# Where three groups of low parts are formed: a pointwise weight of the convolution layer behind its sixth chunk, and four splits at the end of attention on GpSimd instead of VectorE

## The chip, the cores and the metric

The kernel runs on one core of a Trainium2 chip. The time is the device time of one execution in microseconds; runs are compared by their medians. The five engines named below are TensorE (PE, with its weight loads as PEld), VectorE (DVE), ScalarE (ACT), GpSimd (POOL) and SyncE (SP, which here only issues transfers).

## The reference

A trunk of two layers works on 512 tokens of width 1024, all in float32. Layer 0 mixes tokens with a Conformer convolution, layer 1 with differential attention of 8 heads. After each mixer stand a SwiGLU FFN and a gated per-layer input `p` of width 256.

```python
def conformer_conv(x, ...):
    a = x @ w_pw1 + b_pw1
    u = a[..., :D] * sigmoid(a[..., D:])
    u = conv_general_dilated(u, dw_w, causal, width 31) + dw_b
    u = silu(layer_norm(u, ln_g, ln_b))
    return u @ w_pw2 + b_pw2

def diff_attention(x, ...):
    q, k, v = split(x @ w_qkv, 3)
    q = rms_norm(q, q_g) * HEAD_DIM ** -0.5;  k = rms_norm(k, k_g)
    # per block of 128 queries, per head
    probs = softmax(q @ k.T + bias, causal)          # two maps per head
    w = probs[:, :, 0] - lam * probs[:, :, 1]
    o = rms_norm(w @ v, sub_g) * (1 - lambda_init)
    return o @ w_o
```

The projection of `p` (`p @ ple_w_proj`, 256 to 1024) doesn't depend on the mixer, so the kernel can do it anywhere in a layer.

## The kernel before

The stream is kept transposed as 8 chunks of 128 features by 512 tokens. Each float32 product is made of three TensorE products: a factor is split into a high part (a rounded copy) and a low part (the value minus the high part), and `mm3` (L160 to L166) adds low by high, high by low and high by high. A weight of 128 by 1024 therefore takes three steps (`weight`, L146): a transfer into one of two `wraw` buffers, ACT's copy `whi` (L157), and a subtraction that gives `wlo` (L159), on DVE unless `eng` says otherwise. The same is done to activations: `z` in the convolution layer (L571 on ACT, L575 on DVE), the attention outputs `A` (L178, L179), and the two halves of `p` (`pfeatures`, L278 and L279).

Each engine works through its own instructions in a fixed order. A planner sets that order when the program is built; in the loop over `z` the order of DVE and ACT is that of the code, and `issue_after` puts an instruction behind another one. An instruction whose operands aren't ready holds up everything behind it on its engine.

Two places matter here.

**The start of the second pointwise product (`w_pw2`, about 150 to 182 us).** For each of 8 chunks DVE shifts (L550, or POOL at L560 for chunks 3 to 7) and multiplies (L568), ACT does silu (L569) and the high part (L571), DVE the low part (L575). `linear` starts three output blocks together, so that each chunk of `z` feeds three weights; the fourth weight follows alone. The planner had put the fourth weight's split among the first chunks.

**The end of attention (about 755 to 805 us).** Work is cut into stages. A unit multiplies tokens by a slab of the q and k weights, scales the result on POOL by the root found there (`r`, L229; `big<-big,r`, L925), and `unit_end` transposes it on PE (L931) and writes the six `C` tiles on ACT, DVE and POOL (L939 to L949). `stage_s` makes the scores (PE L976, L977), which DVE reads from one of two `sc` buffers (L979), ACT exponentiates (L983) and DVE combines (L986 to L988). `stage_t` transposes them (PE L996) and splits them (ACT L998, DVE L999). `stage_a` multiplies by the values (PE L1012, L1013), `stage_o` transposes the outputs (PE L1041). When the last slab is done, the loop over `pp` fills in the projection of `p`: `project` multiplies two weights (`w = weight()`, each used for four output blocks) by the two halves of `p`, with a stage between the pieces.

For a narrow block of queries both maps share one `sc` buffer, so that the second map's matmuls wait until DVE has read the first.

Of the kernel before, what the change touches and what calls it, by code (L numbers as in the profile page):

```python
# [15 lines left out]
ALU = mybir.AluOpType  # L16
# [4 lines left out]
P = 128  # L21
S = 512
D = 1024
NC = D // P
# [68 lines left out]
def trunk(ctx, tc, xT, pT, wts, diag, dww, vec, rel, onehot, lamv, out):  # L93
    nc = tc.nc
    V, A, G, T = nc.vector, nc.scalar, nc.gpsimd, nc.tensor
# [20 lines left out]
    f = lambda ap: ap.bitcast(F32)  # L116
# [6 lines left out]
    def col(name, i=0):  # L123
        a, _ = VEC[name]
        return vt[:, a + i : a + i + 1]
# [17 lines left out]
    wnext = [0]  # L143
    loaded = [None]

    def weight(n=1024, pieces=1, between=(), eng=V, after=None):  # L146
        i = wnext[0]
        wnext[0] += 1
        raw = sb([P, 1024], "wraw", 2)
        hi = sb([P, 1024], "whi", 4, F32R)  # L150
        lo = sb([P, 1024], "wlo", 4, F32R)
        for k in range(pieces):
            cut = slice(k * n // pieces, (k + 1) * n // pieces)
            loaded[0] = nc.sync.dma_start(raw[:, cut], wts[i, :, cut])
            if k < len(between):
                between[k]()
            A.copy(hi[:, cut], raw[:, cut])  # L157
            with tc.issue_after(after.ins) if after else nullcontext():
                eng.tensor_tensor(lo[:, cut], raw[:, cut], f(hi[:, cut]), ALU.subtract)  # L159
        return hi, lo  # L160
# [7 lines left out]
    def wpart(w, k):  # L168
        return tuple(t[:, k * P : (k + 1) * P] for t in w)
# [98 lines left out]
    def pfeatures(layer, parts):  # L268
        for k, (hi, lo) in enumerate(parts):
            if layer == 0:  # L270
                if k == 0:
                    two = sb([P, 2, S], "B7", 1)
                    nc.sync.dma_start(two.rearrange("p a s -> p (a s)"), pT[layer])
                raw = two[:, k]
            else:
                raw = sb([P, 1024], "wraw", 2)[:, :S]
                nc.sync.dma_start(raw, pT[layer, :, k * S : (k + 1) * S])
            A.copy(hi, raw)  # L278
            (G if layer == 0 else V).tensor_tensor(lo, raw, f(hi), ALU.subtract)  # L279
        return parts  # L280


# [11 lines left out]
    y = []  # L294
# [141 lines left out]
    last_add = [None]  # L436
# [77 lines left out]
    def factor(after):  # L514
        m = len(pp)
        if m < 6:
            o = sb([P, S], f"D{m}", 1)
        elif m == 6:
            pw.append(sb([P, 2, S], "C4", 2))
            o = pw[2][:, 0]  # L520
        else:
            o = pw[2][:, 1]
        with tc.issue_after(after[0].ins):
            pp.append(project(ph, m, pw[m // 4], o))
# [34 lines left out]
        for c in range(3, NC):  # L559
            G.tensor_tensor(y[c], y[c], drow, ALU.add)  # L560

    z = []
    with tc.manual_schedule(engines={V.engine, A.engine}):
        for c in range(NC + 1):
            if c < NC:
                if c in (1, 2):
                    shift(c)
                V.tensor_tensor(y[c], y[c], lrow, ALU.mult)  # L568
                A.activation(y[c], y[c], AF.Silu, scale=col("ln_g", c), bias=col("ln_b", c))  # L569
                z.append((sb([P, S], f"A{2 * c}", 1, F32R), sb([P, S], f"A{2 * c + 1}", 1, F32R)))  # L570
                A.copy(z[c][0], y[c])  # L571
                if c < 2:
                    factor(last_product)
            if c >= 1:
                V.tensor_tensor(z[c - 1][1], y[c - 1], f(z[c - 1][0]), ALU.subtract)  # L575

    def linear(n_in, src, consume, group0=1, before=None, after=None, first=(None,) * 3):


        m = 0  # L580
        while m < NC:
            g = group0 if m == 0 else 1
            ws = [weight(n_in * P, after=first[i] if m == 0 else None) for i in range(g)]
            accs = [mm() for _ in range(g)]
            for k in range(n_in):
                if before:
                    before(k)
                for w_, a_ in zip(ws, accs):
                    mm3(a_, wpart(w_, k), src[k], k == 0, k == n_in - 1)
                    if after:  # L590
                        after()
            for i in range(g):
                consume(m + i, accs[i])
            m += g
# [3 lines left out]
    def add_conv(m, acc):  # L598
        V.scalar_tensor_tensor(h[m], acc, col("b_pw2", m), h[m], ALU.add, ALU.add)
        norm.chunk(m)  # L600

    linear(NC, z, add_conv, 3, first=(None, last_add[0], None))


    def ffn(norm, after, space):
# [449 lines left out]
    def take(n):  # L1055
        got, stages[:n] = [s for _, s in stages[:n]], []
        return got

    waiting = None
    for what, at, pace in QKV:  # L1060
        ws = slab(GLO if what == "q" and at > 0 else 0, P * at[1] if what == "v" else S)
        for tb in range(4):
            if (what, at, tb) == ("v", (6, 2), 0):
                ph = pfeatures(1, [both(sb([P, 2, S], t, 1, F32R)) for t in ("B0", "B1")])
            between = take(3 * pace[tb])
# [22 lines left out]
    pp = []  # L1088
    for m in range(NC):
        if m % 4 == 0:  # L1090
            w = weight()
        step()
        if m % 2 == 0:
            o2 = sb([P, 2, S], f"B{m // 2 + 2}", 1) if m < 4 else sb([P, 2, S], f"C{m // 2 + 1}", 2)
        pp.append(project(ph, m, w, o2[:, m % 2], step))
# [155 lines left out]
```

## Time and profile before

| | |
|---|---|
| runs, us | 1257.83, 1261.02, 1260.38 (median 1260.38) |
| profiled execution, us | 1259.05, of which the span 1257.3 |
| busy, share of span | PE 99%, PEld 86%, DVE 72%, ACT 49%, POOL 21% |
| 150 to 182 us: busy of 32.0 | PE 29.95, DVE 19.57, ACT 19.91, POOL 10.47 |
| 754 to 771 us: busy of 17.0 | PE 16.74, DVE 16.75, ACT 14.25, POOL 9.78 |
| 771 to 804 us: busy of 33.0 | PE 28.54, DVE 31.00, ACT 26.81, POOL 4.51 |
| granted TensorE clock | 1.00 in these stretches, 0.95 as the mean of 771 to 804 |

The time of an execution is its span and 1.75 us around it. In the timelines a row has the start, the duration, the engine, the line, the operation with output and inputs, and in brackets how long the engine had stood idle and what ended that. The same form can be longer in one place than in another (a subtraction of 128x1024 on DVE: 1.22 to 2.64 us). Matmuls overlap: three of 128 by 512 in a row start some 0.23 us apart though each lasts 0.40.

### The profile page before, as it was taken

Reading aid. Unit: us, or ns where it says so; the run is one execution under the profiler, and the core shown is the slowest. Engines: PE = TensorE matmul, PEld = TensorE weight load, DVE = VectorE, ACT = ScalarE, POOL = GpSimd, SP = SyncE. Lnnn points to the kernel's source line nnn. Section 1 sums busy time; section 2 is a strip of 40 time slices with the busy share of each in tenths; the row PEclk is TensorE's granted clock in tenths of the full one; section 3 lists DMA queues with packets and bytes.
Section 4 is the critical chain, followed back from the end, with each engine's and each line's share of the span. In section 5 each row is a group of like instructions: output and inputs, shape, how many; then the busy total and the mean of one; then the engine's idle time right before and its main releaser. Section 6 shows DMA issues by size and latency. Waiting matters only on the chain.

```text
span 1257.3 us, 18628 instructions
## 1 busy us (share of the span) xinstructions
PE 1239.1 (99%) x7152; PEld 1086.2 (86%) x7152; DVE 904.6 (72%) x1482; ACT 615.5 (49%) x1023; POOL 264.1 (21%) x231
## 2 busy tenths in 40 slices
PE   9999999999999999999999998999999999999998
PEld 7888778898999899988888987878898999899887
DVE  6998755965588558667678889746965598468665
ACT  6743454543355235446566768634542355235441
POOL 2853522000001000042616633122000000000030
PEclk9999999999999999999999999999999999999999
DMA  8666223464466444243322214223554467444241
GB/s 298 199 194 179 74 76 109 131 164 129 122 176 181 137 110 122 67 147 96 90 92 76 76 48 129 85 67 101 151 156 145 103 182 184 137 109 117 77 134 67
DMA packets 60597, 158.39 MB, mean 126 GB/s; under 512 B 6451, under 2 KB 11059, under 8 KB 60508
## 3 DMA queue, kind: packets, MB, share of 16 engines
q1 hardware_dynamic: 53776, 136.99, 34.3%
q0 software_dynamic: 4608, 16.78, 8.2%
q10 hardware_dynamic: 2124, 3.43, 0.9%
q8 instruction: 56, 0.92, 0.3%
q14 instruction: 33, 0.27, 0.1%
HBM read 151.91 MB, written 4.21 MB: 124 GB/s over the span
## 4 chain that ended last, share of the span: by engine, by line
PE 96%; DVE 2%; ACT 1%; DMA 0%; issue 0%; SPq 0%; ACTq 0%
PE mm L164 26%; PE mm L165 25%; PE mm L166 25%; PE tp L166 2%; PE tp L165 2%; PE tp L164 2%; PE sc L370 2%; PE sc L165 1%; PE sc L166 1%; PE sc L164 1%; PE mm L1012 1%; PE sc L976 1%; PE sc L977 1%; PE tp L996 1%; PE mm L370 1%; PE mm L326 1%
## 5 line engine op out<-in xcount | busy, mean ns | idle before, releaser
L165 PE MATMUL mm<-A,whi 128*128 128x512 f32 (+1 forms) x904 | 311.6, 346 | 0.3 <-DVE A L575 0.3
L164 PE MATMUL mm<-A,wlo 128*128 128x512 f32 (+1 forms) x904 | 307.2, 345 | 4.7 <-DVE wlo L159 3.0
L166 PE MATMUL mm<-A,whi 128*128 128x512 f32 (+1 forms) x904 | 310.0, 343 | 0.0
L157 ACT CAST whi<-wraw 128x1024 fp32r<-128x1024 f32 (+2 forms) x150 | 151.3, 1015 | 225.4 <-PE mm L166 103.8
L159 DVE TENSOR_TENSOR wlo<-wraw,whi 128x1024 fp32r<-128x1024 f32 (+2 forms) x147 | 186.3, 1270 | 61.0 <-ACT whi L157 60.3
L164 PEld LDWEIGHTS mm<-A,wlo 128*128 128x128 f32 x904 | 171.4, 190 | 26.3 <-ACT A L178 2.5
L165 PEld LDWEIGHTS mm<-A,whi 128*128 128x128 f32 x904 | 171.5, 190 | 21.8 <-issue 1.2
L166 PEld LDWEIGHTS mm<-A,whi 128*128 128x128 f32 x904 | 171.6, 190 | 20.8 <-issue 1.4
L165 PE MATMUL mm<-B,whi 128*128 128x512 f32 x368 | 143.3, 390 | 0.0
L166 PE MATMUL mm<-B,whi 128*128 128x512 f32 x368 | 143.3, 390 | 0.0
L164 PE MATMUL mm<-B,wlo 128*128 128x512 f32 x368 | 141.1, 391 | 0.0
L681 POOL DMA_DIRECT2D C<-in_wts x32 | 28.1, 878 | 512.1 <-DVE h L792 178.2
L204 POOL TENSOR_TENSOR acc<-acc,wk 128x512 f32<-128x512 f32 x35 | 56.6, 1617 | 218.3 <-ACT wk L203 110.9
L166 PEld LDWEIGHTS mm<-B,whi 128*128 128x128 f32 x368 | 69.1, 188 | 15.0
L165 PEld LDWEIGHTS mm<-B,whi 128*128 128x128 f32 x368 | 69.1, 188 | 14.3
L164 PEld LDWEIGHTS mm<-B,wlo 128*128 128x128 f32 x368 | 69.1, 188 | 14.2
L166 PE MATMUL mm<-whi,A 128*128 128x512 f32 (+1 forms) x224 | 81.1, 363 | 0.0
L164 PE MATMUL mm<-whi,A 128*128 128x512 f32 (+1 forms) x224 | 80.9, 366 | 0.0
L165 PE MATMUL mm<-wlo,A 128*128 128x512 f32 (+1 forms) x224 | 80.8, 364 | 0.0
L792 DVE TENSOR_TENSOR h<-mm,h 128x512 f32<-128x512 f32 x48 | 33.0, 688 | 64.5 <-PE mm L166 64.5
L229 POOL TENSOR_TENSOR r<-v,mhalf 128x8 f32<-128x8 f32 (+1 forms) x31 | 46.2, 1490 | 120.9 <-DVE v L227 99.9
L674 DVE TENSOR_TENSOR wlo<-wraw,whi 128x1024 fp32r<-128x1024 f32 x32 | 39.2, 1225 | 33.5 <-ACT whi L673 33.4
(271 smaller groups left out, 2674.4 us busy)
## 6 DMA issues: line engine op xcount, KB each, us to landing
wraw<-in_wts SPq DMA_DIRECT2D x162, 512.0 KB, 3.6
C<-in_wts SPq DMA_DIRECT2D x32, 512.0 KB, 4.8
C<-in_wts POOLq DMA_DIRECT2D x32, 512.0 KB, 5.8
bias<-in_wts SPq DMA_DIRECT2D x32, 256.0 KB, 3.2
wraw<-in_wts SPq DMA_DIRECT2D x16, 384.0 KB, 3.1
D<-in_diag SPq DMA_DIRECT2D x22, 256.0 KB, 4.6
C<-in_diag SPq DMA_DIRECT2D x16, 256.0 KB, 4.7
h<-in_xT SPq DMA_DIRECT2D x8, 256.0 KB, 5.4
```

Source lines behind the costliest of these rows:

```text
L157: A.copy(hi[:, cut], raw[:, cut])
L159: eng.tensor_tensor(lo[:, cut], raw[:, cut], f(hi[:, cut]), ALU.subtract)
L164: T.matmul(acc, al, bh, start=first, stop=False)
L165: T.matmul(acc, ah, bl, start=False, stop=False)
L166: return T.matmul(acc, ah, bh, start=False, stop=last)
L204: self.last = self.eng.tensor_tensor(self.acc, self.acc, sq, ALU.add)
L229: last_pow[0] = G.tensor_tensor(r[:, :n], v[:, :n], mhalf[:, :n], ALU.pow)
L326: last_tap[0] = T.matmul(acc, dg[:, j % 4], ups[c][:, j : j + S], start=(j == 0), stop=(j == PE_TAPS[c] - 1))
L370: last_tap[0] = T.matmul(acc[:, g * P : (g + 1) * P], w, ups[c][:, g, LEAD - m : LEAD - m + P], start=(m == 0), stop=(m == LAGS - 1),)
L674: V.tensor_tensor(lo, raw, f(hi), ALU.subtract)
L681: nc.gpsimd.dma_start(q, wts[i + 2].rearrange("p (a s) -> p a s", a=2), accum_op=ALU.add)
L792: V.tensor_tensor(h[m], acc, h[m], ALU.add)
```

## The change

Three edits. (1) `weight()` gets `behind`, which puts ACT's copy after a named instruction, and `linear` uses it for the first weight after the starting group: in `w_pw2` the fourth weight's copy now comes after the high part of the sixth chunk, and its subtraction after that chunk's low part. (2) The low parts of the two halves of `p` for layer 1 are subtracted on POOL instead of DVE. (3) So are the low parts of the two weights of the projection of `p` at the end of attention.

```diff
-    def weight(n=1024, pieces=1, between=(), eng=V, after=None):
+    def weight(n=1024, pieces=1, between=(), eng=V, after=None, behind=None):
...
-            A.copy(hi[:, cut], raw[:, cut])
+            with tc.issue_after(behind.ins) if behind else nullcontext():
+                A.copy(hi[:, cut], raw[:, cut])
             with tc.issue_after(after.ins) if after else nullcontext():
                 eng.tensor_tensor(lo[:, cut], raw[:, cut], f(hi[:, cut]), ALU.subtract)
...
-            (G if layer == 0 else V).tensor_tensor(lo, raw, f(hi), ALU.subtract)
+            G.tensor_tensor(lo, raw, f(hi), ALU.subtract)
...
-                A.copy(z[c][0], y[c])
+                z_hi.append(A.copy(z[c][0], y[c]))
...
-                V.tensor_tensor(z[c - 1][1], y[c - 1], f(z[c - 1][0]), ALU.subtract)
+                z_lo.append(V.tensor_tensor(z[c - 1][1], y[c - 1], f(z[c - 1][0]), ALU.subtract))
...
-    def linear(n_in, src, consume, group0=1, before=None, after=None, first=(None,) * 3):
+    def linear(n_in, src, consume, group0=1, before=None, after=None, first=(None,) * 3, then=(None, None)):
...
-            ws = [weight(n_in * P, after=first[i] if m == 0 else None) for i in range(g)]
+            if m == group0:
+                ws = [weight(n_in * P, behind=then[0], after=then[1])]
+            else:
+                ws = [weight(n_in * P, after=first[i] if m == 0 else None) for i in range(g)]
...
-    linear(NC, z, add_conv, 3, first=(None, last_add[0], None))
+    linear(NC, z, add_conv, 3, first=(None, last_add[0], None), then=(z_hi[5], z_lo[5]))
...
         if m % 4 == 0:
-            w = weight()
+            w = weight(eng=G)
```

Line numbers of the changed kernel are 1 to 4 higher. In the rows below a name has a buffer number and then running numbers; `B0` to `B7` in the first place are the eight chunks before the split, `A0, A1` to `A14, A15` their high and low parts.

DVE at the start of `w_pw2`, before:

```order
L575 TENSOR_TENSOR A1_272_1396<-B0_93_381,A0_271_1395 128x512
L550 SCALAR_TENSOR_TENSOR B2_140_652<-tp_249_1288,B2_140_652 128x512
L568 TENSOR_TENSOR B2_140_652<-B2_140_652,tp_269_1382 128x512
L159 TENSOR_TENSOR wlo_313_1579<-wraw_311_1577,whi_312_1578 128x1024
L575 TENSOR_TENSOR A3_276_1411<-B1_115_536,A2_275_1410 128x512
L568 TENSOR_TENSOR B3_161_801<-B3_161_801,tp_269_1382 128x512
L575 TENSOR_TENSOR A5_279_1426<-B2_140_652,A4_278_1425 128x512
```

and now, from the same multiplication of the third chunk on:

```order
L569 TENSOR_TENSOR B2_140_652<-B2_140_652,tp_269_1382 128x512
L576 TENSOR_TENSOR A3_276_1411<-B1_115_536,A2_275_1410 128x512
L569 TENSOR_TENSOR B3_161_801<-B3_161_801,tp_269_1382 128x512
L576 TENSOR_TENSOR A5_279_1426<-B2_140_652,A4_278_1425 128x512
L569 TENSOR_TENSOR B4_187_920<-B4_187_920,tp_269_1382 128x512
L576 TENSOR_TENSOR A7_281_1432<-B3_161_801,A6_280_1431 128x512
L569 TENSOR_TENSOR B5_210_1080<-B5_210_1080,tp_269_1382 128x512
L576 TENSOR_TENSOR A9_283_1438<-B4_187_920,A8_282_1437 128x512
L569 TENSOR_TENSOR B6_227_1206<-B6_227_1206,tp_269_1382 128x512
L576 TENSOR_TENSOR A11_285_1444<-B5_210_1080,A10_284_1443 128x512
L569 TENSOR_TENSOR B7_240_1251<-B7_240_1251,tp_269_1382 128x512
L160 TENSOR_TENSOR wlo_313_1579<-wraw_311_1577,whi_312_1578 128x1024
```

The weight's subtraction has moved from behind the third chunk's multiplication to behind the eighth's. ACT's copy of it moves likewise, from between silu and high part of the second chunk to behind the high part of the sixth. On PE the fourth weight's products, which began after the first three products of the second chunk, begin after those of the seventh.

POOL at the end of attention, before (`C2` and `C3` are tiles of k, `D3` a head's output, `big_1379` the last unit's q and k):

```order
L944 CAST C3_1297_7001<-C3_1297_7001 64x2x128
L229 TENSOR_TENSOR r8_1361_7300<-v8_1360_7298,mhalf_4_71 128x4
L944 CAST C2_1296_7000<-C2_1296_7000 64x2x128
L944 CAST C3_1297_7001<-C3_1297_7001 64x2x128
L1034 TENSOR_TENSOR D3_1328_7133<-D3_1328_7133,r8_1361_7300 128x512
L229 TENSOR_TENSOR r8_1383_7398<-v8_1382_7396,mhalf_4_71 128x8
L925 TENSOR_TENSOR big_1379_7390<-big_1379_7390,r8_1383_7398 128x512
```

and now:

```order
L948 CAST C3_1297_7001<-C3_1297_7001 64x2x128
L280 TENSOR_TENSOR B0_1390_7413<-wraw_1392_7415,B0_1390_7413 128x512
L280 TENSOR_TENSOR B1_1391_7414<-wraw_1393_7419,B1_1391_7414 128x512
L230 TENSOR_TENSOR r8_1361_7300<-v8_1360_7298,mhalf_4_71 128x4
L948 CAST C2_1296_7000<-C2_1296_7000 64x2x128
L948 CAST C3_1297_7001<-C3_1297_7001 64x2x128
L1038 TENSOR_TENSOR D3_1328_7133<-D3_1328_7133,r8_1361_7300 128x512
L230 TENSOR_TENSOR r8_1383_7398<-v8_1382_7396,mhalf_4_71 128x8
L160 TENSOR_TENSOR wlo_1428_7652<-wraw_1426_7650,whi_1427_7651 128x1024
L160 TENSOR_TENSOR wlo_1488_7869<-wraw_1486_7867,whi_1487_7868 128x1024
L929 TENSOR_TENSOR big_1379_7390<-big_1379_7390,r8_1383_7398 128x512
```

The two halves of `p` (`B0`, `B1`) stand ahead of a head's root, and both weights of the projection stand between the last unit's root and its scaling.

PE there, before (`tp_1402` is the last unit's transposes, `sc_1420` the last scores of one head, `sc_1446` the first of the next, `mm_1404` and `mm_1429` products with the values):

```order
L931 MATMUL tp_1402_7475<-ident_2_65,big_1379_7390 128x128 x4
L976 MATMUL sc_1420_7587<-C3_1192_6466,C1_1190_6464 128x512
L977 MATMUL sc_1420_7587<-C5_1194_6468,C1_1190_6464 128x512
L996 MATMUL tp_1409_7527<-ident_2_65,big_1373_7347 128x128
L1013 MATMUL mm_1404_7499<-B4_1260_6829,wtl_1401_7460 128x128
L1012 MATMUL mm_1404_7499<-B5_1269_6887,wth_1400_7459 128x256
L1013 MATMUL mm_1404_7499<-B5_1269_6887,wtl_1401_7460 128x128
L1012 MATMUL mm_1404_7499<-B6_1271_6915,wth_1400_7459 128x256
L1013 MATMUL mm_1404_7499<-B6_1271_6915,wtl_1401_7460 128x128
L1012 MATMUL mm_1404_7499<-B7_1281_6971,wth_1400_7459 128x256
L1013 MATMUL mm_1404_7499<-B7_1281_6971,wtl_1401_7460 128x128
L976 MATMUL sc_1446_7703<-C2_1296_7000,C0_1294_6998 128x128
```

and now, up to the first product of the projection (`mm_1443`):

```order
L1017 MATMUL mm_1404_7499<-B7_1281_6971,wtl_1401_7460 128x128
L980 MATMUL sc_1454_7740<-C2_1296_7000,C0_1294_6998 128x256
L981 MATMUL sc_1454_7740<-C4_1298_7002,C0_1294_6998 128x256
L935 MATMUL tp_1402_7475<-ident_2_65,big_1379_7390 128x128 x4
L1000 MATMUL tp_1409_7527<-ident_2_65,big_1373_7347 128x128
L980 MATMUL sc_1446_7703<-C3_1297_7001,C1_1295_6999 128x128
L981 MATMUL sc_1446_7703<-C5_1299_7003,C1_1295_6999 128x128
L980 MATMUL sc_1454_7740<-C3_1297_7001,C1_1295_6999 128x256
L981 MATMUL sc_1454_7740<-C5_1299_7003,C1_1295_6999 128x256
L1016 MATMUL mm_1429_7656<-B4_1260_6829,wth_1410_7529 128x256
L165 MATMUL mm_1443_7696<-B0_1390_7413,wlo_1428_7652 128x512
```

The last unit's transposes have moved behind `sc_1420` and the products of `mm_1404`, and the second map of `sc_1446` and both of `sc_1454`, which came after the projection's first twelve products, now come ahead of them.

More of the change, by code (lines that the diff above doesn't have):

```diff
@@ L560, in trunk @@
             G.tensor_tensor(y[c], y[c], drow, ALU.add)
-    z = []
+    z, z_hi, z_lo = [], [], []
     with tc.manual_schedule(engines={V.engine, A.engine}):
```

## The prediction

> **What bounds the kernel now.** I read the page's busy times and chain first, then PE's waits, then the timeline at the two places that the change touches.
>
> ```profile
> PE 1239.1 (99%) x7152; PEld 1086.2 (86%) x7152; DVE 904.6 (72%) x1482; ACT 615.5 (49%) x1023; POOL 264.1 (21%) x231
> ...
> PE 96%; DVE 2%; ACT 1%; DMA 0%; issue 0%; SPq 0%; ACTq 0%
> ```
>
> TensorE is the bound: 99% busy and 96% of the chain. A change elsewhere is worth only what it takes from PE's waits, and those are few:
>
> ```profile
> PE sc L976 <- DVE st L979: 3.3, 4, 1.6
> PE mm L164 <- DVE wlo L159: 3.0, 2, 1.8
> PE mm L1012 <- ACT wth L998: 2.0, 2, 1.1
> ```
>
> (us in all, times, longest.) One of the two waits for `wlo` stands at the start of `w_pw2`, the other at 835 us, which the change doesn't reach. Most of the first and all of the third group stand at the end of attention.
>
> **The start of `w_pw2`.** PE, then DVE and POOL:
>
> ```profile
> 155.91 0.50 PE L165 MATMUL mm<-A,whi 128*128 128x512 f32 x1 [0.34 <-DVE A L575]
> ...
> 157.42 0.86 PE L164 MATMUL mm<-A,wlo 128*128 128x512 f32 x3
> 159.49 0.47 PE L164 MATMUL mm<-A,wlo 128*128 128x512 f32 x1 [1.22 <-DVE wlo L159]
> ```
>
> ```profile
> 154.39 1.46 DVE L575 TENSOR_TENSOR A<-B,A 128x512 fp32r<-128x512 f32 x1 [0.22 <-ACT A L571]
> ...
> 157.09 2.25 DVE L159 TENSOR_TENSOR wlo<-wraw,whi 128x1024 fp32r<-128x1024 f32 x1
> 159.27 0.68 DVE L575 TENSOR_TENSOR A<-B,A 128x512 fp32r<-128x512 f32 x1
> ```
>
> ```profile
> 151.51 6.75 POOL L560 TENSOR_TENSOR B<-B,wk 128x512 f32<-128x512 f32 x5 [1.95 <-ACT wk L558]
> ```
>
> Three products start 0.23 us apart (0.86 for three that last 0.40 each), so the one after 157.42 would have started at 158.11: it came 1.38 late, for the fourth weight's low part. That subtraction took 2.25, beside POOL's last shift, which ran to 158.26. The low part of the first chunk at 154.39 took 1.46 beside POOL too, and a later one 0.68 alone.
>
> The change takes both steps of the fourth weight out of this place. Next in line on DVE at 157.09 is then the low part of the second chunk, which PE now needs at 158.11 too. It has two operands in SBUF like the instruction that it replaces, so by the same row it doesn't get through before POOL's shift ends at 158.26. It ends near 158.9, and PE waits about 0.8 instead of 1.38: a gain of 0.6. If POOL lets it through at once it ends at 157.8 and all 1.38 is gained. The wait of 0.34 before it stays. Nothing is late further on: a chunk costs PE three weights by three products, 9 x 0.23 = 2.1 us, and ACT and DVE make one in 1.4 or less (0.62 + 0.82 on ACT), so the fourth weight's split, at the end of the sixth chunk's on ACT, is done some 2 us ahead of the seventh chunk's first products. I take -0.6, with -1.4 and 0 as ends.
>
> **What a subtraction costs on POOL, and what it does to DVE.** Two places of the trace have a DVE instruction with two SBUF operands beside POOL's split of a weight, and one has a DVE instruction that reads PSUM beside POOL's scaling:
>
> ```profile
> 642.80 2.41 POOL L159 TENSOR_TENSOR wlo<-wraw,whi 128x1024 fp32r<-128x1024 f32 x1 [6.20 <-issue]
> ...
> 643.65 2.64 DVE L159 TENSOR_TENSOR wlo<-wraw,whi 128x1024 fp32r<-128x1024 f32 x1 [1.14 <-ACT whi L157]
> ```
>
> ```profile
> 708.28 2.40 POOL L159 TENSOR_TENSOR wlo<-wraw,whi 128x1024 fp32r<-128x1024 f32 x1 [0.62 <-ACT whi L157]
> ```
>
> ```profile
> 709.34 1.37 DVE L987 SCALAR_TENSOR_TENSOR st<-st,lam 128x1 f32<-128x1 f32 x1
> ```
>
> ```profile
> 757.59 0.49 DVE L947 SCALAR_TENSOR_TENSOR C<-tp,lam,C 64x256 fp32r<-64x256 f32 x1
> 757.61 1.04 POOL L925 TENSOR_TENSOR big<-big,r 128x512 f32<-128x512 f32 x1
> ```
>
> The split takes POOL 2.40. In both cases DVE's instruction ended when POOL's had, plus its own work: 643.65 + 2.64 is 1.08 after 645.21, and the combination of one column, a matter of 0.2 us, lasted until 710.71, POOL's end being 710.68. The one from PSUM lost nothing. So of 2.40 on POOL DVE lost 1.4 and 1.2. [...]
>
> **The end of attention.** What leaves DVE, and what stands around it:
>
> ```profile
> 760.24 0.16 DVE L1030 TENSOR_TENSOR v<-v,r 128x4 f32<-128x4 f32 x1
> 760.32 1.29 DVE L279 TENSOR_TENSOR B<-wraw,B 128x512 fp32r<-128x512 f32 x2
> 761.52 0.16 DVE L227 TENSOR_SCALAR v<-v 128x4 f32<-128x4 f32 x1
> ...
> 767.73 2.99 DVE L159 TENSOR_TENSOR wlo<-wraw,whi 128x1024 fp32r<-128x1024 f32 x2
> 771.03 0.54 DVE L979 CUSTOM_DVE_ANT_0 acc<-sc,bias 128x384 f32<-128x384 f32 x1
> 771.51 0.68 DVE L999 TENSOR_TENSOR wtl<-tp,wth 128x512 fp32r<-128x512 f32 x1
> ...
> 775.42 0.48 DVE L988 SCALAR_TENSOR_TENSOR big<-rb,st,big 128x256 f32<-128x256 f32 x1
> ...
> 776.23 1.21 DVE L159 TENSOR_TENSOR wlo<-wraw,whi 128x1024 fp32r<-128x1024 f32 x1
> ```
>
> POOL, and ACT's second copy of a weight, which had waited 0.75 for its transfer:
>
> ```profile
> 758.72 0.40 POOL L944 CAST C<-C 64x256 fp32r<-64x256 f32 x1
> ...
> 765.75 1.64 POOL L229 TENSOR_TENSOR r<-v,mhalf 128x8 f32<-128x8 f32 x1
> 767.46 1.04 POOL L925 TENSOR_TENSOR big<-big,r 128x512 f32<-128x512 f32 x1
> ```
>
> ```profile
> 767.10 1.05 ACT L157 CAST whi<-wraw 128x1024 fp32r<-128x1024 f32 x1 [0.75 <-DMA wraw<-in_wts]
> ```
>
> PE, and the clock in one stretch (us, then busy and instructions by engine, then the granted clock):
>
> ```profile
> 770.14 0.60 PE L931 MATMUL tp<-ident,big 128*128 128x128 f32 x4
> 771.64 0.50 PE L976 MATMUL sc<-C,C 128*128 128x512 f32 x1 [0.90 <-DVE st L979]
> ...
> 774.55 0.39 PE L1012 MATMUL mm<-B,wth 128*128 128x256 f32 x1 [0.94 <-ACT wth L998]
> ...
> 779.98 0.38 PE L1012 MATMUL mm<-B,wth 128*128 128x256 f32 x1 [1.06 <-ACT wth L998]
> ...
> 781.85 1.06 PE L1041 MATMUL tp<-ident,D 128*128 128x128 f32 x4 [0.52 <-DVE wtl L999]
> ...
> 788.58 0.40 PE L164 MATMUL mm<-B,wlo 128*128 128x512 f32 x1
> ```
>
> ```profile
> 781.90:785.30 3.40, 3.40 (x14) 3.10 (x15) 2.74 (x11) 1.66 (x5) 0.00 (x0) 0.50 0.35 133
> ```
>
> The four waits quoted come to 3.4 us, and DVE stands behind all of them: it has no gap here. The halved clock costs 3.4 x 0.5 = 1.7 more. So relief of DVE would be paid in full, if it came: 1.2 for the halves of `p` (760.32 to 761.52) and 2.9 for the two weights (767.73 to 770.64, the next row's start being the end), 4.1 in all.
>
> *The halves of `p`.* On POOL 128 by 512 costs half of 2.40, 1.2, against 1.04 for the scaling (757.61): I take 1.2. POOL is free at 759.12, so they run to 760.3 and 761.5. DVE's L227 would come at 760.4, but it is one of those that a two-operand POOL instruction holds up, and POOL's next root waits for POOL's own end anyway. DVE goes on at 761.5, where it stood before. Term: 0, with -1.2 as the lower end.
>
> *The two weights, step by step.* POOL's root starts some 0.6 later than at 765.75, since DVE now reads a score ahead of the sum, and ends at 768.0; the splits run 768.0 to 770.4 and, after DVE's turn, to 773.2. The scaling of the last unit, done at 768.5 before, ends at 774 to 775. The transposes that need it stand behind `mm_1404` on PE, whose products wait for DVE's split of 128 by 512 (done at 772.1, next sentences), so PE reaches them at 773.2: a wait of 1.8 at the later end, and the score matmuls are behind it. DVE has the 2.9 back at 767.73, and loses it again: after one score (768.6) it combines 128 by 256 (0.48) behind POOL's first split and is at 770.9, reads the next score (0.67), splits (0.68), adds a slab's part (0.48) and is at 772.7; the next combination of a column waits for the second split, 773.3. Then come two combinations (0.6 and 0.75), a score, the slab's other part, a sum, a reduction (0.7 each at most) and another weight (1.21): the score that `sc_1446` needs read first is done at 778.5. PE, finished with the transposes at 775.4, waits 3.0 for it, and starts the projection after the small scores at 779.3 instead of 774.77. But these scores, and the waits of 779.98 to 781.85 around them, lie behind it then: twelve products of 0.23 end at 782.1. From there to the second twelve PE has 4.6 us of work (the rows between 777.55 and 788.58 without the scores already done and at full clock), and DVE, 3 us of products ahead by then, holds it up by 2 to 3 more. The second twelve start at 788.7 to 789.7, against 788.58. I take +0.6 in the middle, and ends of -4.1 (DVE keeps all that it is given) and +5 (below).
>
> No transfer is moved past another that matters: both raw weights keep their buffers, and the halves' raw buffers come free at 760.3 and 761.5 instead of 760.9 and 761.5.
>
> **Sum.** -0.6 + 0 + 0.6 = 0 on 1259.05, the profiled execution, which is 1.33 under the median of the runs. Against the median: 1260.4. About 0.3%, 3.8 us, is what a measurement of this kernel can tell from no change.
>
> **The rivals.** *DVE's relief is real* (faster). If POOL's splits fall into DVE's PSUM reads, as at 757.59, DVE keeps most of the 4.1, the 0.90 and 0.94 and what follows go, and PE reaches the second twelve 3.5 to 4.1 earlier. With -0.6 to -1.4: about 1255.5. For it: DVE reads PSUM in most of its rows here. Against: a column's combination between them is enough to stop it, as at 709.34.
>
> *POOL's queue and the clock* (slower). PE stands 1.8 and 3.0 us with little between, 773.2 to 778.5. Before, waits of 0.90 to 1.06 were followed by 3.4 us at half clock. If the clock halves once more, the walk has +1.7, and if the column's combination at 767.9 also falls behind the first split, DVE loses up to 2.4 that PE then waits for: +4.1 on the sum, 1264.5. It decides from the point at which the splits have begun before DVE's column is ready, about 767.9. [...]
>
> *Only the first edit counts.* The end of attention comes out even and the second chunk isn't held up: -1.4, 1259.0. It differs from my forecast only within what can be told.
>
> **How the numbers follow.** Forecast 0.50, only the first edit 0.08, relief real 0.23, queue and clock 0.19. Faster 0.23, within 0.3% 0.58, slower 0.19. The range reaches to the cases on both sides, 1255 to 1265; the likeliest one's own is 1257 to 1263.
>
> **What would show it.** At 159 us: a wait of about 0.8 on L166 for DVE's low part in place of 1.22 for `wlo`, or none. At 760: DVE's L228 over 1 us long. At 768 to 773: two POOL splits of 2.4, and DVE combinations of one column or 256 that last over 1.3. At 774: PE's transposes of the last unit waiting for POOL, then scores waiting for DVE until about 778. I am wrong if DVE's durations beside the splits stay as they were, or if the projection's first product starts before 777.

## The result, and the profile after

The changed kernel is slower: 1266.02 us (median of 6 runs, 1264.82 to 1268.26) against 1259.85 for the kernel before in the same set of runs (6 runs), a ratio of 1.0054 [1.0043, 1.0064]. The profiled execution took 1266.09, its span 1264.3. The forecast was no change, with 1265 as the upper end. The page's busy times and chain, and PE's waits:

```profile
PE 1241.8 (98%) x7152; PEld 1088.0 (86%) x7152; DVE 908.7 (72%) x1478; ACT 617.3 (49%) x1023; POOL 271.8 (21%) x235
...
PE 94%; DVE 3%; ACT 1%; issue 1%; DMA 0%; SPq 0%; ACTq 0%; DVEq 0%
```

```profile
PE sc L980 <- DVE st L983: 8.7, 7, 3.2
PE mm L165 <- DVE wlo L160: 1.8, 1, 1.8
```

The waits for DVE's reads of scores have grown from 3.3 to 8.7 us; one of the two for `wlo` is gone. DVE is busy for longer than before although four of its subtractions left it (x1478 against x1482), and POOL got 7.7 us for them.

Where the time went is read from rows that both kernels have. PE, after, then before (four transposes of one unit ahead of the end of attention, and the first products of the SwiGLU layer that wait for a weight):

```profile
753.77 0.63 PE L935 MATMUL tp<-ident,big 128*128 128x128 f32 x4
...
842.25 0.50 PE L165 MATMUL mm<-A,wlo 128*128 128x512 f32 x1 [1.75 <-DVE wlo L160]
```

```profile
753.31 0.63 PE L931 MATMUL tp<-ident,big 128*128 128x128 f32 x4
...
835.49 0.50 PE L164 MATMUL mm<-A,wlo 128*128 128x512 f32 x1 [1.75 <-DVE wlo L159]
```

Between the two rows lie 88.48 us after and 82.18 before: the end of attention lost 6.30. By the same reading `w_pw2` gained 0.62: equal rows of PE are 1.07 late at 120 to 150 us and 0.45 late from 185 us on. (The 1.07 comes from the first 20 us, 3.41 us at a granted clock of 0.50 from 8.56 on, in which the trace of before has 1.00.) From 842 us to the end only 0.26 more is lost.

**The start of `w_pw2`.** PE, then DVE, after:

```profile
156.97 0.50 PE L166 MATMUL mm<-A,whi 128*128 128x512 f32 x1 [0.32 <-DVE A L576]
...
159.93 0.50 PE L166 MATMUL mm<-A,whi 128*128 128x512 f32 x1 [0.59 <-DVE A L576]
```

```profile
158.16 1.71 DVE L576 TENSOR_TENSOR A<-B,A 128x512 fp32r<-128x512 f32 x1
...
166.05 1.22 DVE L160 TENSOR_TENSOR wlo<-wraw,whi 128x1024 fp32r<-128x1024 f32 x1
```

The second chunk's low part now stands where the weight's stood, it is held up by POOL's shift (1.71 instead of 0.68, to 159.87, where the shift ran to 159.32), and PE waits 0.59 for it instead of 1.22 for `wlo`.

**The end of attention.** POOL, DVE and PE, after:

```profile
759.66 2.87 POOL L280 TENSOR_TENSOR B<-wraw,B 128x512 fp32r<-128x512 f32 x2
...
768.93 4.74 POOL L160 TENSOR_TENSOR wlo<-wraw,whi 128x1024 fp32r<-128x1024 f32 x2
773.62 1.24 POOL L929 TENSOR_TENSOR big<-big,r 128x512 f32<-128x512 f32 x1
```

```profile
761.41 1.15 DVE L228 TENSOR_SCALAR v<-v 128x4 f32<-128x4 f32 x1
...
769.05 2.31 DVE L991 SCALAR_TENSOR_TENSOR st<-st,lam 128x1 f32<-128x1 f32 x1
...
771.76 2.20 DVE L992 SCALAR_TENSOR_TENSOR big<-rb,st,big 128x256 f32<-128x256 f32 x1
...
780.34 1.22 DVE L160 TENSOR_TENSOR wlo<-wraw,whi 128x1024 fp32r<-128x1024 f32 x1
...
781.76 0.28 DVE L983 CUSTOM_DVE_ANT_0 big<-sc,bias 128x128 f32<-128x128 f32 x1
```

```profile
774.62 0.33 PE L980 MATMUL sc<-C,C 128*128 128x128 f32 x1 [1.42 <-DVE st L983]
...
777.07 0.58 PE L980 MATMUL sc<-C,C 128*128 128x256 f32 x1 [0.83 <-DVE st L983]
...
777.66 1.06 PE L935 MATMUL tp<-ident,big 128*128 128x128 f32 x4
...
782.10 0.47 PE L980 MATMUL sc<-C,C 128*128 128x128 f32 x1 [3.17 <-DVE st L983]
...
783.34 0.63 PE L165 MATMUL mm<-B,wlo 128*128 128x512 f32 x1
...
794.87 0.39 PE L165 MATMUL mm<-B,wlo 128*128 128x512 f32 x1
```

The first split on POOL began at 768.93, 0.12 ahead of DVE's combination of one column. That combination, 0.21 before, lasted 2.31, the next one 2.20 instead of 0.48: both ended within 0.3 of the end of one of POOL's two splits (near 771.3 and at 773.67). The read of `sc_1446`'s first map came at 781.76, and PE, which has its second map next, waited for it. The last two rows are the first products of the projection's first and second twelve. The windows of 3.41 us around it, with the granted clock behind the five engines, after and before:

```profile
773.15:776.56 3.41, 1.50 (x10) 1.16 (x9) 3.38 (x9) 1.18 (x3) 1.71 (x2) 1.00 0.76 246
776.56:779.97 3.41, 1.86 (x7) 1.46 (x7) 2.79 (x8) 2.30 (x5) 0.00 (x0) 0.50 0.41 91
779.97:783.39 3.42, 1.29 (x6) 1.29 (x7) 3.29 (x11) 3.35 (x8) 1.82 (x3) 0.50 0.29 39
783.39:786.80 3.41, 3.41 (x10) 2.64 (x10) 3.35 (x14) 2.34 (x9) 0.39 (x2) 0.50 0.29 118
```

```profile
775.06:778.48 3.42, 3.42 (x22) 2.89 (x20) 3.36 (x11) 2.38 (x8) 0.00 (x0) 1.00 0.08 8
778.48:781.89 3.41, 1.36 (x8) 0.79 (x7) 3.41 (x11) 3.01 (x8) 0.00 (x0) 1.00 0.88 243
```

PE ran at half clock for 10.24 us, against 3.41 before; nine of the projection's first twelve products fall into the last window, where they start 0.43 us apart (0.23 at full clock).

### The profile page after: what moved, and what is told of

Its sections match the earlier page's. It is cut to its first block, busy times and chain, and to the rows that moved or that the text cites. A ratio compares the mean times of both kernels' runs of the same rounds, so it can differ in the third digit from the quotient of the medians.

```text
span 1264.3 us, 18616 instructions
## 1 busy us (share of the span) xinstructions
PE 1241.8 (98%) x7152; PEld 1088.0 (86%) x7152; DVE 908.7 (72%) x1478; ACT 617.3 (49%) x1023; POOL 271.8 (21%) x235
## 4 chain that ended last, share of the span: by engine, by line
PE 94%; DVE 3%; ACT 1%; issue 1%; DMA 0%; SPq 0%; ACTq 0%; DVEq 0%
PE mm L165 25%; PE mm L166 25%; PE mm L167 25%; PE tp L167 2%; PE tp L166 2%; PE tp L165 2%; PE sc L371 2%; PE sc L166 1%; PE sc L167 1%; PE sc L165 1%; PE mm L1016 1%; PE sc L980 1%; PE mm L371 1%; PE sc L981 1%; PE tp L1000 1%
## 5 line engine op out<-in xcount | busy, mean ns | idle before, releaser
L160 DVE TENSOR_TENSOR wlo<-wraw,whi 128x1024 fp32r<-128x1024 f32 (+2 forms) x145 | 182.4, 1261 | 60.1 <-ACT whi L158 59.4
```

## The experiments

Theory after the result: POOL's two splits hold up DVE's combinations (called the reads below and 'port' in the expectations; both are names, no run shows what the two engines share), and that costs the 6.3. Rivals: POOL's longer queue makes the last unit's scaling late; the planner's new order of rows is worse by itself; the clock. The table has every run but `lock_alone`, which does other work behind the kernel; "ratio" compares with the kernel before in the same set of runs, with a 95% interval; "end" is the change in the distance between the two PE rows above, in the run's own trace (one execution), and "half clock" the us at 0.50 between 770 and 800 in it.

| run | ratio to before | end, us | half clock |
|---|---|---|---|
| the change | 1.0054 [1.0043, 1.0064] | +6.3 | 10.2 |
| e1_pw2 | 0.9999 [0.9989, 1.0008] | -0.4 | 3.4 |
| e2_halves | 0.9999 [0.9989, 1.0009] | -0.9 | 0 |
| e12_pw2_halves | 0.9998 [0.9989, 1.0008] | -0.9 | 0 |
| e3_weights | 1.0034 [1.0022, 1.0045] | +3.5 | 6.8 |
| f_pinned | 1.0048 [1.0031, 1.0065] | +6.6 | 10.2 |
| f_pieces4 | 1.0039 [1.0026, 1.0052] | +4.4 | 10.2 |
| g_nosplit | 1.0019 [1.0009, 1.0029] | +3.5 | 10.2 |
| x_before_nosplit | 0.9993 [0.9983, 1.0004] | -1.7 | 0 |
| x_after_nosplit | 1.0025 [1.0016, 1.0034] | +3.0 | 6.8 |
| x_after_fill | 1.0025 [1.0014, 1.0035] | +2.6 | 6.8 |
| x_before_pool_ahead | 1.0024 [1.0013, 1.0035] | +2.6 | 6.8 |
| x_before_pool_behind | 1.0010 [0.9999, 1.0021] | +1.7 | 6.8 |
| y_best | 1.0003 [0.9994, 1.0012] | +0.6 | 3.4 |
| y_wth | 0.9989 [0.9980, 0.9997] | -0.7 | 3.4 |
| y_wth_dve | 0.9998 [0.9989, 1.0007] | +0.4 | 6.8 |

**One edit at a time.** `e1_pw2` has the first edit alone, `e2_halves` and `e3_weights` a line each, `e12_pw2_halves` the first two edits.

```diff
e1, e12: +    linear(NC, z, add_conv, 3, first=(None, last_add[0], None), then=(z_hi[5], z_lo[5]))
e2, e12: +            G.tensor_tensor(lo, raw, f(hi), ALU.subtract)
e3:      +            w = weight(eng=G)
```

> The first edit alone: the attention end is the kernel before, row for row. In the changed kernel's trace the wait of 1.22 us for the fourth weight at the start of w_pw2 became one of 0.59 for the second chunk's low part, and PE's rows gain 0.62 us across this place. All theories: about 0.6 us faster than before, which is inside what can be told (within 0.3%). If it is over 2 us faster or slower, the first edit does something that the two traces don't show.

> The second edit alone (the low parts of p's halves on GpSimd). Theory 'port': DVE is given 1.2 us and loses 1.0 to 1.5 of it again, since its two-operand rows wait for POOL's subtractions; result within 1.5 us of before. Theory 'relief': 1 us or more faster. Theory 'order' (the planner's new row order at the end of attention costs by itself, whichever engine splits): 2 us or more slower, with DVE's rows at their ordinary lengths.

> The third edit alone (the two projection weights' low parts on GpSimd). Theory 'port': carries nearly all of the loss, 4 to 7 us slower than before, with one DVE combination of a column and one of 128x256 at 1.5 to 2.4 us beside POOL's two splits, PE waiting over 3 us for a score that DVE reads late, and two or three windows at half clock instead of one. Theory 'queue' (the last unit's scaling stands behind the splits on POOL): the same loss, but PE's largest wait is that of the last unit's transposes for POOL. Theory 'sum of all three edits': 1 to 3 us slower.

> The first two edits, the weights' splits back on DVE. Theory 'port': the loss goes with POOL's two splits, within 1.5 us of the kernel before (1258.2 to 1261), since pw2's gain of 0.6 is left and the halves come out even. Theory 'sum of edits' (the halves cost 2 us beside the weights, as the difference of the changed kernel to the third edit alone suggests): 1261 to 1262.5.

The first two edits, alone and together, come out even; in the trace of the first `w_pw2` gains 0.61, too little for the runs to show. With the halves on POOL, DVE's `v<-v` of 4 columns lasted 1.14 (0.16 before), and PE waited 0.34 and 0.49 for the DVE rows behind it, as it does in the change (0.36 and 0.49); before, it waits for nothing there. In these runs that is made up further on, with another order and without a window at half clock. In all three kernels the planner's order at the end of attention differs from that of before, so a new order need not cost anything. The third edit alone carries 1.0034, not all of 1.0054. DVE there, two combinations of a column in one row:

```profile
771.24 3.31 DVE L987 SCALAR_TENSOR_TENSOR st<-st,lam 128x1 f32<-128x1 f32 x2
```

So the loss needs the third edit. That the other two add to it is what the two ratios say; how they do it no run separates.

**POOL's queue: the splits behind the scaling, or in pieces.** `f_pinned` puts both splits behind the last unit's scaling, `f_pieces4` makes each of four pieces.

```diff
f_pinned:  +            w = weight(eng=G, after=last_scaled[0])
f_pieces4: +                for j in range(4):   # 128x256 at a time
```

> The changed kernel with both splits of the projection weights put behind the last unit's scaling on POOL. Theory 'queue': the loss goes, within 1.5 us of the kernel before or faster (1256 to 1261). Theory 'port': the splits still run beside DVE's two-operand rows, which again last up to 2.4 us; 2 to 6 us slower than before (1262 to 1266), though the transposes are on time.

> The changed kernel with each of POOL's two splits cut into four of 128x256. Theory 'port': DVE is let in between the pieces, so a combination of a column lasts at most 0.6 to 0.9 us instead of 2.31 and that of 128x256 at most 1.2 instead of 2.20; half or more of the loss goes, 1260 to 1263. Theory 'POOL's work itself' (queue and order, not the port): POOL is busy as long or longer, 1265 to 1268.

With the scaling done ahead of the splits the time stays. In `f_pinned` POOL's two splits run for 4.90 us from 768.83 on; DVE beside them:

```profile
769.28 2.22 DVE L993 SCALAR_TENSOR_TENSOR big<-rb,st,big 128x256 f32<-128x256 f32 x1
```

In pieces no combination of DVE lasts over 1.06, but POOL's work grows from 4.74 to 6.11 and the kernel stays slower (1.0039). Both kernels also got new rows from the planner, so neither tells queue, reads and order apart. The next runs hold the rows.

**No split at all.** `g_nosplit` is the changed kernel with the two splits left out (the low parts are not formed), in the order that the planner then makes.

> The changed kernel with the two projection weights' splits left out (the high part is multiplied in place of the low part, so the projection of p in layer 1 is computed wrongly): neither DVE nor POOL does that work. It measures what a relief of DVE by 2.9 us would be worth if it cost nothing elsewhere. Theory 'port': 2 to 4.5 us faster than before (1255 to 1258), since DVE is behind every wait here. Theory 'order': the planner's new row order loses by itself, 1261 or more in spite of the work left out.

Without a single split the kernel is still slower than before, 1.0019. What is left is the order (a third one, neither that of before nor that of the change) and the low parts of `p` on POOL.

**Orders held.** In the runs from here on every engine's order at the end of attention is written out, by dependencies without a semaphore from each instruction to the next:

```diff
     ple(n2, pp, store, CUTS)
+    traced = list(nc.cur_bb.bb.instructions)
+    for row in ROWS.values():          # one list of positions for each engine
+        for a_, b_ in zip(row, row[1:]):
+            tc.add_manual_dep(traced[b_], traced[a_].name, ...NoSync..., reason="row")
```

`x_before_nosplit` and `x_after_nosplit` have the rows of before and of after, the two splits left out; `x_after_fill` has the rows of after, with fills of the same length on POOL in the splits' place; `x_before_pool_ahead` the rows of before with the splits on POOL ahead of the last scaling. The rows of after keep the first two edits, the halves of `p` on POOL among them. That holding the rows costs something by itself doesn't show: `y_wth_dve` below, with held rows and both splits on DVE, is even with before.

> The kernel before with every engine's rows pinned to its own order at the end of attention, and only the two projection weights' subtractions left out of DVE's (the high part is multiplied in place of the low part, so the projection of p in layer 1 is computed wrongly). What a relief of DVE by 2.9 us is worth if nothing else moves. Theory 'relief counts': 2 to 4 us faster than before (1255.5 to 1257.5), with PE's waits for scores and for the split transposes shorter. Theory 'relief is worth little' (PE meets the next wait at once, or the clock): within 1 us of before.

> The changed kernel with every engine's rows pinned to its order, and the two subtractions left out of POOL's (again the high part in place of the low part). Theory 'port': the order is harmless, so with POOL's splits gone the time is that of the kernel before or better (1255 to 1260). Theory 'order': still 1262 or more, since PE has the small scores ahead of the projection and waits for DVE there.

> The changed kernel with every engine's rows pinned to its order, and POOL's two subtractions replaced by fills with zeros of about the same length, which write SBUF and read nothing (the projection weights' low parts are zero). POOL's queue is as long as in the changed kernel. Theory 'port': DVE's column combination and that of 128x256 last 0.2 and 0.5 us again, and the result is within 1.5 us of the same kernel with nothing in the splits' place. Theory 'queue': 1264 to 1267 as the changed kernel, with PE waiting for the last unit's scaling.

> The kernel before with every engine's rows pinned to its own order, the two subtractions taken from DVE and put on POOL ahead of the last unit's scaling, where the changed kernel has them. Theory 'port': slower than before by 3 us or more in spite of the old order (1263 or more), DVE losing as much beside the splits as it was relieved of, and the transposes of the last unit late. Theory 'order': within 1.5 us of before.

Four things follow.

*The relief is worth almost nothing.* 2.9 us of work taken off DVE for free, in the old order, give 0.9993, with an interval that includes 1; the medians alone, 1259.90 against 1259.04, would give 1.0007. One trace ends 1.7 earlier, which is what its missing window at half clock is worth by an estimate (3.41 x 0.5). PE waits again:

```profile
774.07 0.39 PE L1013 MATMUL mm<-B,wth 128*128 128x256 f32 x1 [2.17 <-ACT wth L999]
```

The same wait was 0.94 before: DVE comes earlier, ACT doesn't. This is the row of before from which ACT works without a gap up to the copy `wth` (774.24):

```profile
770.78 0.47 ACT L939 ACTIVATE C<-tp,lam 64x256 fp32r<-64x256 f32 x1 [0.54 <-PE tp L931]
```

ACT stands there behind PE's transposes of the last unit, not behind DVE, and without the splits the transposes and this row start 0.41 earlier, which is how much earlier (0.42) that whole trace runs.

*The new order costs.* The rows of after, without splits, give 1.0025, about 3 us more than before and 4 more than the old rows without splits. The halves of `p` on POOL (and the first edit) are part of these rows; by themselves, in `e2_halves` and `e12_pw2_halves`, they cost nothing, but in these rows they weren't put back on DVE. PE and DVE of `x_after_nosplit`:

```profile
779.61 0.47 PE L981 MATMUL sc<-C,C 128*128 128x128 f32 x1 [3.78 <-DVE st L984]
```

```profile
775.66 0.16 DVE L991 RECIPROCAL st<-st 128x1 f32<-128x1 f32 x1 [0.55 <-ACT rb L988]
...
778.04 1.22 DVE L161 TENSOR_TENSOR wlo<-wraw,whi 128x1024 fp32r<-128x1024 f32 x1
...
779.26 0.28 DVE L984 CUSTOM_DVE_ANT_0 big<-sc,bias 128x128 f32<-128x128 f32 x1
```

DVE stands 0.55 for ACT here, yet the read that PE needs is behind a slab's combination, a sum and a weight's split in its row. PE has the second map of `sc_1446` ahead of the twelve products of the projection, which in the old order came first. An order of after with these products moved ahead wasn't tried.

*POOL being busy costs nothing in that order.* Fills for 4.85 us give the 1.0025 of no work at all, though the scaling is as late as in the change:

```profile
769.35 4.85 POOL L162 MEMSET wlo<- 128x1024 f32 x6
774.17 1.04 POOL L933 TENSOR_TENSOR big<-big,r 128x512 f32<-128x512 f32 x1
```

*What is left is the reads.* The same rows with splits instead of fills are the change itself: 1.0054 against 1.0025, +6.3 against +2.6 in the traces. Beside the fills DVE's combinations have their usual length (0.22 and 0.48 where the change has 2.31 and 2.20). The splits also free the weights' raw buffers later than the fills do, but in the trace of the change neither PE nor ACT waits for a transfer between 766 and 800 us.

In the old order the queue is waited for: with the splits ahead of the scaling PE's transposes wait for it, and DVE's combinations, which come later there, lose little (the longest takes 0.51).

```profile
773.56 0.66 PE L931 MATMUL tp<-ident,big 128*128 128x128 f32 x4 [2.82 <-POOL big L925]
```

**The reads by themselves.** `lock_alone` adds, behind the last result of the kernel before, 14 DVE instructions beside three splits on POOL: combinations of one column, then products that read PSUM, then the combinations beside fills.

> The kernel before with a tail behind its result: 14 column combinations on DVE beside POOL subtractions of 128x1024, then 14 products of 128x128 from PSUM and SBUF beside the same, then 14 column combinations beside POOL fills of 128x1024, which write and read nothing. Theory 'port': in the first part a combination lasts over 2 us whenever a subtraction has begun ahead of it, in the second and third none is over 0.5 us. Theory 'GpSimd slows DVE in general': the second part shows it too, with products of 1 us or more. About 35 us longer than before in all.

POOL and DVE:

```profile
1257.16 7.22 POOL L1142 TENSOR_TENSOR wlo<-wraw,whi 128x1024 fp32r<-128x1024 f32 x3 [37.91 <-DVE whi L1132]
...
1275.86 8.02 POOL L1146 MEMSET wlo<- 128x1024 f32 x8
```

```profile
1257.38 2.19 DVE L1137 COPY st<-wk 128x6 f32<-128x6 f32 x1
1259.61 7.84 DVE L1151 SCALAR_TENSOR_TENSOR st<-st 128x1 f32<-128x1 f32 x14
...
1267.83 4.52 DVE L1149 TENSOR_TENSOR wk<-mm,wk 128x128 f32<-128x128 f32 x14
...
1275.36 3.52 DVE L1151 SCALAR_TENSOR_TENSOR st<-st 128x1 f32<-128x1 f32 x14
```

Beside fills 14 combinations take 3.52; beside splits 7.84. The 4.32 more fit into the second and the third split, which run from about 1259.6 to 1264.38. The products from PSUM are done in 4.52, 0.32 each, while the splits run on for 2.7 more: none of them stood for a split. So in this run the combinations, whose inputs are all in SBUF, stood for subtractions (7.84) and not for fills (3.52), and the products with one input in PSUM didn't stand for subtractions (0.32 each).

**The splits behind the scaling, in the old order.** `x_before_pool_behind` has neither the new rows nor a late scaling; `y_best` adds the first edit to it.

> The kernel before with every engine's order at the end of attention held as it was, only that the two subtractions of the projection's weights leave VectorE and stand on GpSimd behind the last unit's scaling. It has neither the new order of rows nor a later scaling; what is left is the reading of GpSimd beside VectorE's combinations, and the 2.9 us that VectorE is given. Theory 'order first, reads second': VectorE loses most of the 2.9 again (a combination of 1.1 or more beside the splits), PE's waits there stay near those of before, 1259 to 1261. Rival 'the reads alone': the two splits cost VectorE 3.7 whatever the order, PE waits for it, 1262 to 1264. Rival 'relief pays once the queue is right': 1256 to 1258.

> The first edit (the fourth weight of the second pointwise product behind the sixth chunk) together with the end of attention in the order of before and the two subtractions on GpSimd behind the last scaling; the halves of p stay on VectorE. Theory: -0.6 from the first edit on whatever the other form gives, 1258 to 1260. Rival 'the reads alone': 1261 to 1263. Rival 'relief pays once the queue is right': 1255 to 1257, a version that beats both kernels.

Both come out even within their intervals (1.0010 [0.9999, 1.0021] and 1.0003 [0.9994, 1.0012]); with the splits ahead of the scaling it was 1.0024 [1.0013, 1.0035], which overlaps with the first of them. DVE loses 1.75 of its 2.9 again (a column's combination of 1.96 in one, 1.94 in the other), but PE's wait is for ACT. ACT and PE of `y_best`, then ACT of before:

```profile
774.29 1.04 ACT L158 CAST whi<-wraw 128x1024 fp32r<-128x1024 f32 x1 [1.16 <-DMA wraw<-in_wts]
775.36 0.27 ACT L1002 CAST wth<-tp 128x128 fp32r<-128x128 f32 x1
```

```profile
775.68 0.38 PE L1016 MATMUL mm<-B,wth 128*128 128x256 f32 x1 [3.44 <-ACT wth L1002]
```

```profile
773.16 1.05 ACT L157 CAST whi<-wraw 128x1024 fp32r<-128x1024 f32 x1
774.24 0.27 ACT L998 CAST wth<-tp 128x128 fp32r<-128x128 f32 x1
```

The third weight is loaded into the buffer that the first split frees. On POOL that split ends near 770.7 (half of the 4.72 that begin at 768.38), on DVE it ended near 769.2. A transfer of such a weight takes 3.5 us there (the median of four from 764 to 785 us in `y_best`), so it lands at 774.2 instead of 772.7; ACT waits for it, and PE waits 3.44 behind ACT.

**That wait taken away.** `y_wth` is `y_best` with ACT's copy of the third weight behind the 128x128 copy and an exponential; `y_wth_dve` is the same order with both splits on DVE.

```diff
-   'Activation': [..., 6445, 6049, 6096, ...]     # whi of the third weight, wth, exponential
+   'Activation': [..., 6049, 6096, 6445, ...]
```

> As the run y_best, and on ScalarE the copy of the third weight at the end of attention stands behind the slab's rounded copy (128x128) and one exponential instead of ahead of them. In y_best that weight's transfer waits for GpSimd's first split to free its buffer, lands 1.2 us after ScalarE was ready, and TensorE waits 3.44 for the 128x128 copy behind it. Theory 'the buffer is freed late': the wait of 3.44 shrinks to about 1, the end of attention gains 1.5 to 2.3, 1257 to 1258.5. Rival 'given back': VectorE's reads come next and the time stays at 1259 to 1260.

> The same order on ScalarE with both subtractions on VectorE, as in the kernel before (and the first edit). It tells what the reordering on ScalarE alone is worth: before, TensorE waits 0.94 at this place without any wait for a transfer. Theory: the 0.94 goes and is partly given back, 1258 to 1259.5, so that GpSimd's help would be worth the difference to y_wth, 0.5 to 1.5. Rival 'the relief is worth nothing': both within 0.5 of each other.

`y_wth` is faster than the kernel before by 0.1% (1258.45 against 1260.06 in the same set of runs), `y_wth_dve` isn't. PE and ACT of `y_wth`:

```profile
774.01 0.39 PE L1016 MATMUL mm<-B,wth 128*128 128x256 f32 x1 [1.23 <-ACT wth L1002]
...
780.84 0.38 PE L1016 MATMUL mm<-B,wth 128*128 128x256 f32 x1 [1.75 <-ACT wth L1002]
```

```profile
774.85 1.05 ACT L158 CAST whi<-wraw 128x1024 fp32r<-128x1024 f32 x1 [0.18 <-DMA wraw<-in_wts]
```

The 3.44 is down to 1.23, and a later wait for `wth`, 1.75, is new, so less than the 2.2 is kept. This is the lowest ratio of all, with the splits on POOL that come with a loss of 0.5% in the change. The first edit and the new order on ACT are in it too, and `y_wth_dve`, with the splits on DVE, has an interval that overlaps with its own: that POOL's help gains anything isn't shown.

## Why the prediction was wrong

**`w_pw2`, -0.6: right.** -0.61 and -0.62 in two traces, by the mechanism described (0.59 of wait where 0.8 was forecast, the low part held up by POOL's shift).

**The halves of `p`, 0: right in the runs that have this edit without the third, and partly by luck.** L228 did last over 1 us (1.15), and `e2_halves` and `e12_pw2_halves` come out even. The pair took 2.87 on POOL, not 2.4, and PE waited 0.36 and 0.49 for the DVE rows behind L228; the walk had no such wait, nor what made up for it. What the halves cost beside the weights wasn't measured.

**The weights, +0.6: the term that failed.** The end of attention measured +6.3, and +3.5 in the trace with the third edit alone. Three steps of the walk were wrong:

1. *The read that `sc_1446` needs "is done at 778.5".* It was done at 782.04; less the 0.46 by which this trace runs late, 3.1 later than forecast. The walk put the column's combination at 767.9, ahead of POOL's first split, and let DVE lose 1.8 to that split and 0.5 to the second. The combination came at 769.05 (0.7 later, less the 0.46), 0.12 behind the split's start, and two rows in turn were blocked for 2.1 and 1.7 more than their own work: 3.8 instead of 2.3. With the 0.7 and the 1.5 between 3.8 and 2.3 that leaves 0.9 of the 3.1, mostly a wait of DVE for ACT's exponential (0.55), which the walk didn't have. The rival *POOL's queue and the clock* had one whole split of 2.40 as its price (2.4 more) and named the point that decides, about 767.9, but got 0.19. PE's wait of 1.8 for POOL's scaling never came: the scaling ended at 774.86, and PE, after waits of 0.56, 1.42 and 0.83 for scores, was at the transposes at 777.66, 4.0 later than in the walk (773.2, less the 0.46).
2. *The small scores "lie behind it then", and PE regains almost 4 us.* The projection started 8.1 late (783.34 against 774.77 + 0.46) and its second twelve 5.8 late (794.87 against 788.58 + 0.46): 2.3 regained, where the walk had 3.9. Part of the difference is the clock, left out of the sum: three windows at half speed instead of one. In the trace they hold 6.56 us of PE's busy time against 3.41 before, which at full clock would be about half (products of 128 by 512 start 0.43 apart there and 0.23 at full clock): by this estimate 3.3 against 1.7, so 1.6 more. The rows of after, held without the weights' splits, cost 3.0 in their trace; the walk made the new order pay for itself.
3. *"So relief of DVE would be paid in full", 4.1.* With 2.9 of it given for free, the runs show 0.9 us (0.9993), at best 2.1 (0.9983). That DVE has no gap doesn't make its time PE's time, and it didn't stand behind all four waits: the 0.94 at 774.55 was for ACT's copy `wth`, and ACT had worked without a gap since 770.78, behind PE's transposes. This wait, next in line, was not costed. It also takes away the mechanism of the faster rival.

*"No transfer is moved past another that matters"* was wrong too, though the changed kernel hides it: a split that ends 1.5 later on POOL frees its raw buffer 1.5 later, and in the old order PE waits behind that.

By the held rows the 1.0054 is made of about 0.0025 for the new order, with the first two edits in it, and 0.0029 for the reads. The second is a difference of two ratios whose intervals are 0.002 wide, and the clock is inside both. Not separated: how much of the order's share is the clock or the halves of `p`, and what the new order would cost with the splits still on DVE.

## What to carry to other kernels

An engine without a gap that everything waits for is not yet worth relieving (here 2.9 us taken off it gave 0.9993 [0.9983, 1.0004]): take the work away for free first, and see which wait comes next. A move of two instructions between engines also makes the planner write another order, and here the new rows cost about as much as the move, while other new orders (`e1_pw2`, `e12_pw2_halves`) cost nothing; compare the two with the rows held. Before work goes to GpSimd, look at what VectorE does just then: in these traces rows that read PSUM pass (a score's read of 128x384 took 0.55 beside the second split in the change, 0.54 before), and rows with two SBUF inputs that come behind the start of GpSimd's subtraction stand until near its end, down to a column's combination (0.21 before, 2.31 in the change).

## What the runs showed of the hardware

A DVE instruction of 128 by 1, 0.21 us before, took 2.31 in the change, where it came 0.12 behind the start of POOL's subtraction. A `v<-v` with one input of 4 columns (1.15 in the change, 0.16 before) and a copy of 6 columns (2.19 in `lock_alone`) stood as well.

The granted clock stood at 0.50 for 3.41 us at a time (781.89 to 785.30 before, 783.13 to 786.54 in `y_wth`), or for three times as long (10.24, from 776.56 to 786.80 in the change). Before, the 3.41 us ahead of the halved ones hold 1.36 us of PE's work; after, 1.50; no wait of PE in them is longer than 1.42. In the windows from 766.32 to 773.15 PE was busy for 3.41 and 2.86, and the window behind each ran at 1.00. Within the halved stretch, windows of 1.86 and 1.29 were followed by halved ones, and one of 3.41 by one at 1.00:

```profile
769.73:773.15 3.42, 2.86 (x21) 2.41 (x19) 3.42 (x4) 1.07 (x3) 3.42 (x2) 1.00 0.26 44
...
786.80:790.20 3.40, 3.40 (x25) 3.06 (x24) 3.08 (x10) 1.91 (x4) 0.88 (x1) 1.00 0.56 154
```

So windows in which PE was busy for 40 and 44% were followed by halved ones. Where the line lies the traces don't say: before, the window from 833.08 on holds 1.66 us (49%) and the next one ran at full clock, while in `y_wth` one with 1.77 (779.72) was followed by a halved one.
